# Conv sums in PSUM, weights' low parts and two conv tiles moved to GpSimd, in a one-core Conformer block

## The chip, the core and the metric

The kernel runs on one core of a Trainium2 chip. The core has a matrix engine (TensorE, in the profile PE, with its weight loads as PEld), a vector engine (VectorE, DVE), an activation engine (ScalarE, ACT), a general engine (GpSimd, POOL) and a queue engine that issues most of the transfers (SyncE, SP). Each works through its own queue in order and waits on semaphores for the others. Data lie in SBUF (128 partitions) and, for matrix results, in PSUM (8 banks of 128 x 512 float32). The metric is the device time of one execution, in microseconds.

## The reference

One layer of a block with two branches and a feed-forward part, sequence 1024, width 1024, all float32. What matters here is the convolution branch:

```python
def causal_depthwise_conv(u, w, b):
    width, ch = w.shape
    out = lax.conv_general_dilated(
        u, w[:, None, :].astype(u.dtype), window_strides=(1,), padding=[(width - 1, 0)],
        dimension_numbers=('NWC', 'WIO', 'NWC'), feature_group_count=ch)
    return out + b.astype(u.dtype)
...
        h = rms_norm(x, norm1_g[l])
        z = h @ w_in[l].astype(h.dtype)
        glu_in, q, k, v, gate_logits = jnp.split(z, SPLITS, axis=-1)

        a_val, a_gate = jnp.split(glu_in, 2, axis=-1)
        a = a_val * jax.nn.sigmoid(a_gate)
        a = causal_depthwise_conv(a, conv_w[l], conv_b[l])
        a = jax.nn.silu(rms_norm(a, conv_norm_g[l]))
        y_a = a @ w_conv_out[l].astype(a.dtype)
```

The convolution has 31 taps for each of 1024 channels. Beside it stand normalised queries and keys, attention in three dilated windows with 16 heads, gates that mix both branches, an output product, and a feed-forward part with a gated three-tap convolution.

## The kernel before

**Exact products from split numbers.** Every float32 matrix product is made of three products of rounded parts. A matrix is split by `split` (L76): ACT copies it into a rounded type (`hi`), DVE subtracts that from the source (`lo`), and the three matmuls hi·hi, hi·lo and lo·hi follow. A weight piece of 128 x 1024 goes through `wpiece` (L92): `stage` (L81) loads it through SP's queue into one of four `raw` buffers, `wsplit` (L86) writes it into one of four `whi` and one of four `wlo` buffers.

**Order of the work.** The program is written as a stream; the framework's planner (`schedule_with_timeline_sim=True`, L1278) orders the instructions of each engine in advance by durations of its own, earlier lines of the program first where several are ready. In blocks under `manual_schedule` (the start, L347, attention, L652, and part of the feed-forward part) ACT, DVE and PE keep the written order. Once planned, each engine's order is fixed.

**Stages.** (1) x is normalised, transposed and split into `hT` (L280 to L417). (2) GLU: for each of eight channel tiles c two products over `hT`, gate (`glug`) and value (`gluv`), each of two halves of 24 matmuls (`gemm_ch`, L115); ACT takes the sigmoid, DVE multiplies into `apad` (L445), a tile with 30 zero columns ahead. (3) q, k, v: six column groups `ch`, each with four weight pieces `qkv` (L512) and eight token tiles of 24 matmuls (`gemm_tok`, L120); for q and k `qkv_head` squares, sums and forms 1/sqrt (a power on POOL, L103, in `rstd_of`), DVE scales into `qn`, and `qkv_tail` transposes four blocks on PE (L496), splits and stores them. v is split and stored. (4) `cover` runs steps of the gate products (L542), (5) attention with the rest of the gate and conv-output products as filling between its steps (`fill`), (6) merge and output product, (7) feed-forward.

**The convolution** (`conv_branch`, L450) is written after the first `cover`, and what it needs is ready much earlier, so its instructions fill DVE's free places in stages 2 and 3. For each tile c: one `tensor_scalar` (L458, tap 0 with the bias) and thirty `scalar_tensor_tensor` (L461), each reading a shifted `apad` and the running sum `cacc`, both in SBUF. ACT then squares the finished tile (L468) and DVE adds it to `sqacc` (L469). When all eight are in, PE sums over channels (`pss`, L551), POOL forms the root (`crs`), PE spreads it (`psr`), DVE scales (L568), ACT takes the SiLU (L569), SP stores to `da` (L570). Attention's tiles (`p`, L589) lie where the convolution's tiles lay, so its first DVE step waits for that store.

**Buffers.** PSUM: pool `psA`, two tiles of two banks (`big_ps`), pool `psB`, four banks (`bank_ps`). GLU products and q/k transposes lie in `psA`, q/k/v and gate products in `psB`. SBUF: `apad` and `cacc` share ten buffers.

Of the kernel before, what the change touches and what calls it, by code (L numbers as in the profile page):

```python
# [13 lines left out]
F32 = mybir.dt.float32  # L14
F32R = mybir.dt.float32r
AF = mybir.ActivationFunctionType
# [5 lines left out]
P = 128  # L22
# [14 lines left out]
SHARE = 0.6  # L37
COVER = (24, 8, 20)


# [12 lines left out]
def block_kernel(ctx: ExitStack, tc: tile.TileContext, x, g1, g2, pack, mask,  # L53
# [21 lines left out]

    def split(hi, lo, src):  # L76

        act.activation(hi, src, AF.Copy)  # L78
        dve.tensor_tensor(out=lo, in0=src, in1=hi.bitcast(F32), op=ALU.subtract)  # L79

# [4 lines left out]

    def wsplit(src, name):  # L86
        hi = wp.tile([P, 1024], F32R, tag="whi", bufs=4, name=f"hi_{name}")[:, : src.shape[1]]
        lo = wp.tile([P, 1024], F32R, tag="wlo", bufs=4, name=f"lo_{name}")[:, : src.shape[1]]
        split(hi, lo, src)
        return hi, lo  # L90

    def wpiece(src, name, raw=None):  # L92
        raw = stage(src, name) if raw is None else raw
        hi, lo = wsplit(raw, name)
# [20 lines left out]
    def gemm_ch(ps, w, actT):  # L115
        for half in range(2):
            for _ in gemm_half(ps[:, half * 512 : half * 512 + 512], w, actT, half):
                pass
# [160 lines left out]
    with tc.tile_pool(name="ph1", bufs=1) as p1:  # L279
# [4 lines left out]
        for tt in range(8):  # L284
            xx = p1.tile([P, CW - 1 + T], F32, tag="apad", bufs=10, name=f"x_{tt}")[:, 0:T]
# [138 lines left out]
        with tc.issue_after(ends[0].ins), tc.issue_after(ends[1].ins):  # L424
            wsecond = [wpiece(w_ch[9], "g1"), wpiece(w_ch[1], "v1")]


        apad = []
        for c in range(8):
            a = p1.tile([P, CW - 1 + T], F32, tag="apad", bufs=10, name=f"apad_{c}")  # L430
            pool.memset(a[:, : CW - 1], 0.0)
# [7 lines left out]
            else:  # L439
                gp = big_ps(f"glug_{c}")  # L440
                gemm_ch(gp, wsecond[0] if c == 1 else wpiece(w_ch[8 + c], f"g{c}"), hT)
                act.activation(sg, gp, AF.Sigmoid)
                vp = big_ps(f"gluv_{c}")
                gemm_ch(vp, wsecond[1] if c == 1 else wpiece(w_ch[c], f"v{c}"), hT)
                dve.tensor_tensor(out=a[:, CW - 1 :], in0=vp, in1=sg, op=ALU.mult)  # L445
            apad.append(a)

        sqacc = p1.tile([P, T], F32, tag="sqacc", bufs=1, name="sqacc")

        def conv_branch():  # L450
            accs = []
            for c in range(8):
                acc = p1.tile([P, CW - 1 + T], F32, tag="apad", bufs=10, name=f"cacc_{c}")[:, 0:T]
                a = apad[c]
                w = lambda j: pk[:, C_CW + c * CW + j : C_CW + c * CW + j + 1]
                for j in range(CW):
                    if j == 0:
                        dve.tensor_scalar(acc, a[:, 0:T], w(0), pk[:, C_CB + c : C_CB + c + 1],  # L458
                                          op0=ALU.mult, op1=ALU.add)
                    else:  # L460
                        dve.scalar_tensor_tensor(out=acc, in0=a[:, j : j + T], scalar=w(j), in1=acc,  # L461
                                                 op0=ALU.mult, op1=ALU.add)
                accs.append(acc)
                if c == 0:
                    act.activation(sqacc, acc, AF.Square)
                else:
                    sq = p1.tile([P, T], F32, tag="csq", bufs=1, name=f"csq_{c}")
                    act.activation(sq, acc, AF.Square)  # L468
                    dve.tensor_tensor(out=sqacc, in0=sqacc, in1=sq, op=ALU.add)  # L469
            return accs  # L470
# [100 lines left out]
        cover(COVER[2])  # L571


# [708 lines left out]
```

## Time and profile before

| what | value |
|---|---|
| median of the runs | 1763.09 us |
| lowest and highest of 3 | 1762.22 and 1764.61 us |
| profiled execution, first to last instruction | 1761.6 us |
| median less that span | 1.5 us |
| matmuls | 8248 |
| HBM traffic | 154 GB/s over the span |

The profile gives the profiled execution by its span; the time around it isn't given apart, and the difference from the median, 1.5 us, is taken for it. The stages in time (us from the span's start): start 0 to 42, GLU 42 to 194, q/k/v 194 to 470, gate products alone 470 to 513, attention 513 to 895, merge and output product 895 to 1075, feed-forward to the end.

In a list of groups a row has the line, the engine, the operation, what it writes and reads, the count, then busy us and mean ns of one, then the engine's idle time just before. In a table by stretches of time a cell is the engine's busy us and, in brackets, its instructions. In a timeline the first two columns are start and duration in us. A matmul's duration contains latency that overlaps with the next matmul, so its rate is read from the distance between starts.

### The profile page before, as it was taken

To read this page: it belongs to the slowest core of one execution; us is meant where nothing else is said; L and a number is where in the kernel's file an instruction comes from. 1 tells how busy PE (TensorE), PEld (TensorE's weight loads), DVE (VectorE), ACT (ScalarE), POOL (GpSimd) and SP (SyncE) were. 2 spreads that over 40 slices of the span, in tenths; PEclk is the share of its full clock that TensorE was granted. 3 is DMA by queue.
4 is the path that set the end of the run, shared out by engine and by line. 5 is a ranking of instruction groups with operands and counts; after the bars stand their busy time and mean duration, and the time that the engine had idled before them with its cause. 6 is when DMAs were issued, how large, how long until landed. Compare 5 with 4: busy or idle time off the path is not lost.

```text
span 1761.6 us, 22662 instructions
## 1 busy us (share of the span) xinstructions
PE 1749.1 (99%) x8248; PEld 1454.3 (83%) x8248; DVE 1329.3 (75%) x1837; ACT 771.7 (44%) x1235; POOL 185.9 (11%) x193
## 2 busy tenths in 40 slices
PE   8999999999999999999999999999999999999999
PEld 6888888888888888888888888888888888888887
DVE  6999999999846666667655564687776777779863
ACT  6111132232256666667564343454544544534431
POOL 1000133034012222222210000000000000000000
PEclk9999999999999999999999999999999999999999
DMA  5111145344585655568446567532222222498851
GB/s 208 48 48 49 42 138 164 123 132 139 179 273 157 179 159 159 161 180 244 139 138 227 173 233 279 207 124 84 84 84 84 77 91 84 128 341 320 292 174 48
DMA packets 146530, 272.79 MB, mean 155 GB/s; under 512 B 11761, under 2 KB 61041, under 8 KB 146418
## 3 DMA queue, kind: packets, MB, share of 16 engines
q1 hardware_dynamic: 145264, 269.24, 47.2%
q10 hardware_dynamic: 1154, 2.10, 0.3%
q8 instruction: 65, 1.06, 0.2%
q14 instruction: 47, 0.39, 0.1%
HBM read 197.90 MB, written 73.40 MB: 154 GB/s over the span
## 4 chain that ended last, share of the span: by engine, by line
PE 93%; DMA 4%; DVE 1%; issue 1%; ACT 1%; SPq 0%; ACTq 0%; DVEq 0%
PE dx L1118 6%; PE xz L850 6%; PE xz L851 6%; PE xz L852 6%; PE qkv L129 5%; PE qkv L127 5%; PE qkv L128 5%; PE dy L1118 4%; PE pp L607 3%; PE gate L110 3%; PE gate L112 3%; PE gate L111 3%; PE y L850 2%; PE y L851 2%; PE y L852 2%; PE o L622 2%
## 5 line engine op out<-in xcount | busy, mean ns | idle before, releaser
L461 DVE SCALAR_TENSOR_TENSOR cacc<-apad,pk,cacc 128x1024 f32<-128x1024 f32 x240 | 299.7, 1288 | 0.7
L79 DVE TENSOR_TENSOR pl<-pp,ph 128x512 fp32r<-128x512 f32 x192 | 100.8, 553 | 88.1 <-ACT ph L78 87.9
L127 PE MATMUL qkv<-hi_qkv,hT 128*128 128x512 f32 x384 | 151.8, 396 | 0.0
L129 PE MATMUL qkv<-hi_qkv,hT 128*128 128x512 f32 x384 | 150.2, 391 | 0.0
L128 PE MATMUL qkv<-lo_qkv,hT 128*128 128x512 f32 x384 | 149.3, 389 | 0.0
L78 ACT ACTIVATE ph<-pp 128x512 fp32r<-128x512 f32 x192 | 87.1, 488 | 121.0 <-PE pp L607 120.3
L592 DVE CUSTOM_DVE_ANT_0 p<-s,m 128x128 f32<-128x128 f32 (+7 forms) x128 | 96.5, 754 | 53.3 <-PE s L588 41.4
L601 POOL TENSOR_SCALAR p<-p,st 128x128 f32<-128x128 f32 (+7 forms) x128 | 97.1, 758 | 315.7 <-DVE st L600 218.7
L1021 DVE SCALAR_TENSOR_TENSOR u<-u,pk 128x1023 f32<-128x1023 f32 x88 | 112.4, 1279 | 1.0 <-ACT u L1019 0.7
L103 POOL TENSOR_TENSOR rs<-ss,mhalf 128x8 f32<-128x8 f32 x32 | 75.0, 2348 | 337.6 <-DVE ss L102 337.6
L110 PE MATMUL gate<-hT,hi_gt 128*128 128x512 f32 x256 | 103.0, 402 | 0.0
L597 ACT ACTIVATE p<-p,st 128x128 f32<-128x128 f32 (+7 forms) x128 | 99.3, 775 | 5.5 <-DVE st L592 4.6
L111 PE MATMUL gate<-hT,hi_gt 128*128 128x512 f32 x256 | 100.3, 392 | 0.0
L112 PE MATMUL gate<-hT,lo_gt 128*128 128x512 f32 x256 | 100.1, 392 | 0.0
L129 PEld LDWEIGHTS qkv<-hi_qkv,hT 128*128 128x128 f32 x384 | 72.1, 188 | 15.3
L79 DVE TENSOR_TENSOR lo_uv<-raw_uv,hi_uv 128x1024 fp32r<-128x1024 f32 x20 | 24.5, 1226 | 79.5 <-ACT hi_uv L78 79.5
L128 PEld LDWEIGHTS qkv<-lo_qkv,hT 128*128 128x128 f32 x384 | 72.2, 188 | 14.3
L607 PE MATMUL pp<-ident,p 128*128 128x128 f32 x576 | 83.8, 272 | 0.0
L127 PEld LDWEIGHTS qkv<-hi_qkv,hT 128*128 128x128 f32 x384 | 72.2, 188 | 13.9
L607 PEld LDWEIGHTS pp<-ident,p 128*128 128x128 f32 x576 | 70.1, 140 | 15.3
L621 PE MATMUL o<-ph,v 128*128 128x512 f32 x192 | 74.8, 393 | 0.7 <-DVE op L633 0.7
L850 PE MATMUL xz<-blk_t,hi_s3g 128*128 128x512 f32 x176 | 68.6, 390 | 0.7 <-ACT xc L995 0.7
(309 smaller groups left out, 4638.8 us busy)
## 6 DMA issues: line engine op xcount, KB each, us to landing
wr<-w_down SPq DMA_DIRECT2D x45, 512.0 KB, 5.5
gr<-dff SPq DMA_DIRECT2D x62, 256.0 KB, 5.2
raw_qkv<-w_qkv SPq DMA_DIRECT2D x24, 512.0 KB, 3.8
dff<-u SPq DMA_DIRECT2D x22, 512.0 KB, 2.6
raw_uv<-w_up SPq DMA_DIRECT2D x21, 512.0 KB, 3.2
raw_ug<-w_up SPq DMA_DIRECT2D x20, 512.0 KB, 3.2
dv<-v SPq DMA_DIRECT2D x16, 512.0 KB, 3.2
raw_gt<-w_ch SPq DMA_DIRECT2D x16, 512.0 KB, 5.2
```

The costliest lines, as they stand in the source:

```text
L110: pe.matmul(o, hi[:, k, :], ah[:, k, :], start=(k == 0), stop=False)
L111: pe.matmul(o, hi[:, k, :], al[:, k, :], start=False, stop=False)
L112: pe.matmul(o, lo[:, k, :], ah[:, k, :], start=False, stop=(k == KT - 1))
L127: pe.matmul(ps, ah, hi[:, k % 2, :], start=(k == 0), stop=False)
L128: pe.matmul(ps, ah, lo[:, k % 2, :], start=False, stop=False)
L129: pe.matmul(ps, al, hi[:, k % 2, :], start=False, stop=(k == KT - 1))
L461: dve.scalar_tensor_tensor(out=acc, in0=a[:, j : j + T], scalar=w(j), in1=acc, op0=ALU.mult, op1=ALU.add)
L607: pe.transpose(pp[:, qb * P : (qb + 1) * P], pts[qb][:, kt * P : (kt + 1) * P], ident)
L850: pe.matmul(o, wh[:, k, :], bh[:, k, :], start=(start and k == 0), stop=False, skip_group_check=not start)
L851: pe.matmul(o, wh[:, k, :], bl[:, k, :], start=False, stop=False, skip_group_check=not start)
L852: end = pe.matmul(o, wl[:, k, :], bh[:, k, :], start=False, stop=(k == 3), skip_group_check=not start)
L1118: pe.matmul(banks[n], a[:, c], b[:, d], start=(start and i == 0 and m == 0), stop=(stop and i == nf - 1 and m == 2), skip_group_check=True)
```

## The change

The running sum of a conv tile moves from SBUF to a PSUM tile `work` of two banks (new pool `psC`, one buffer); the last tap writes the finished tile back over `apad`. For tiles 2 and 5 (`BY_POOL`) ACT makes the tap products (62 in all, alternating between two SBUF buffers) and POOL adds them (60 sums) to `part`. The squares go into `work`, or into a product buffer for tiles 2 and 5, in place of `csq`. The low parts of the weights of the GLU tiles 1 to 7 (14 pieces) and of q, k, v (24 pieces) are subtracted on POOL in place of DVE. The GLU products move from `psA` to the four banks of `psB`, and their sigmoid and product are done by halves. After the GLU stage `psA` is closed; its four banks go to `psC` (two) and `psT` (two tiles of one bank, for the q/k transposes), and are opened again as `psA2` for what follows. `apad` has eight buffers in place of ten.

```diff
+BY_POOL = (2, 5)
...
-    psA = ctx.enter_context(tc.tile_pool(name="psA", bufs=2, space=PSUM))
     psB = ctx.enter_context(tc.tile_pool(name="psB", bufs=4, space=PSUM))
+    psA_cm = tc.tile_pool(name="psA", bufs=2, space=PSUM, reuse_waits="tile")
+    psA = psA_cm.__enter__()
...
-    def split(hi, lo, src):
+    def split(hi, lo, src, by=dve):
 
         act.activation(hi, src, AF.Copy)
-        dve.tensor_tensor(out=lo, in0=src, in1=hi.bitcast(F32), op=ALU.subtract)
+        by.tensor_tensor(out=lo, in0=src, in1=hi.bitcast(F32), op=ALU.subtract)
...
-            wsecond = [wpiece(w_ch[9], "g1"), wpiece(w_ch[1], "v1")]
+            wsecond = [wpiece(w_ch[9], "g1", by=pool), wpiece(w_ch[1], "v1", by=pool)]
...
-                gp = big_ps(f"glug_{c}")
-                gemm_ch(gp, wsecond[0] if c == 1 else wpiece(w_ch[8 + c], f"g{c}"), hT)
-                act.activation(sg, gp, AF.Sigmoid)
-                vp = big_ps(f"gluv_{c}")
-                gemm_ch(vp, wsecond[1] if c == 1 else wpiece(w_ch[c], f"v{c}"), hT)
-                dve.tensor_tensor(out=a[:, CW - 1 :], in0=vp, in1=sg, op=ALU.mult)
+                gp = [bank_ps(f"glug_{c}_{half}") for half in range(2)]
+                gemm_ch(gp, wsecond[0] if c == 1 else wpiece(w_ch[8 + c], f"g{c}", by=pool), hT)
+                vp = [bank_ps(f"gluv_{c}_{half}") for half in range(2)]
+                gemm_ch(vp, wsecond[1] if c == 1 else wpiece(w_ch[c], f"v{c}", by=pool), hT)
+                for half in range(2):
+                    cs = slice(half * 512, half * 512 + 512)
+                    act.activation(sg[:, cs], gp[half], AF.Sigmoid)
+                    dve.tensor_tensor(out=a[:, CW - 1 + half * 512 : CW - 1 + half * 512 + 512],
+                                      in0=vp[half], in1=sg[:, cs], op=ALU.mult)
...
+        psA_cm.__exit__(None, None, None)
+        psC_cm = tc.tile_pool(name="psC", bufs=1, space=PSUM, reuse_waits="tile")
+        psC = psC_cm.__enter__()
+        psT_cm = tc.tile_pool(name="psT", bufs=2, space=PSUM, reuse_waits="tile")
+        psT = psT_cm.__enter__()
...
             accs = []
+            part = p1.tile([P, T], F32, tag="part", name="part")
+            prods = [p1.tile([P, T], F32, tag=t, name=f"prod_{t}") for t in ("prod", "csq")]
             for c in range(8):
-                acc = p1.tile([P, CW - 1 + T], F32, tag="apad", bufs=10, name=f"cacc_{c}")[:, 0:T]
                 a = apad[c]
+                acc = a[:, CW - 1 :]
                 w = lambda j: pk[:, C_CW + c * CW + j : C_CW + c * CW + j + 1]
...
+                bias = pk[:, C_CB + c : C_CB + c + 1]
+                if c in BY_POOL:
+                    act.activation(part, a[:, 0:T], AF.Identity, scale=w(0), bias=bias)
+                    for j in range(1, CW):
+                        act.activation(prods[j % 2], a[:, j : j + T], AF.Copy, scale=w(j))
+                        pool.tensor_tensor(out=acc if j == CW - 1 else part, in0=prods[j % 2], in1=part, op=ALU.add)
+                    work = prods[0]
+                else:
+                    work = psC.tile([P, T], F32, tag="C", name=f"work_{c}")
+                    dve.tensor_scalar(work, a[:, 0:T], w(0), bias, op0=ALU.mult, op1=ALU.add)
+                    for j in range(1, CW):
+                        dve.scalar_tensor_tensor(out=acc if j == CW - 1 else work, in0=a[:, j : j + T], scalar=w(j),
+                                                 in1=work, op0=ALU.mult, op1=ALU.add)
                 accs.append(acc)
                 if c == 0:
                     act.activation(sqacc, acc, AF.Square)
                 else:
-                    sq = p1.tile([P, T], F32, tag="csq", bufs=1, name=f"csq_{c}")
-                    act.activation(sq, acc, AF.Square)
-                    dve.tensor_tensor(out=sqacc, in0=sqacc, in1=sq, op=ALU.add)
+                    act.activation(work, acc, AF.Square)
+                    dve.tensor_tensor(out=sqacc, in0=sqacc, in1=work, op=ALU.add)
...
-            pt = big_ps(f"qt_{ch}_{tt}")[:, 0:512]
+            pt = psT.tile([P, 512], F32, tag="qt", name=f"qt_{ch}_{tt}")
...
-            wpieces = [wpiece(w_qkv[kind * 2 + g8, :, 2 * j : 2 * j + 2, :], f"qkv{ch}_{j}") for j in range(4)]
+            wpieces = [wpiece(w_qkv[kind * 2 + g8, :, 2 * j : 2 * j + 2, :], f"qkv{ch}_{j}", by=pool) for j in range(4)]
...
+    psT_cm.__exit__(None, None, None)
+    psC_cm.__exit__(None, None, None)
+    psA = ctx.enter_context(tc.tile_pool(name="psA2", bufs=2, space=PSUM, reuse_waits="tile"))
```

More of the change, by code (lines that the diff above doesn't have):

```diff
@@ L84, in stage, with wsplit, wpiece @@
         return raw
-    def wsplit(src, name):
+    def wsplit(src, name, by=dve):
         hi = wp.tile([P, 1024], F32R, tag="whi", bufs=4, name=f"hi_{name}")[:, : src.shape[1]]
         lo = wp.tile([P, 1024], F32R, tag="wlo", bufs=4, name=f"lo_{name}")[:, : src.shape[1]]
-        split(hi, lo, src)
+        split(hi, lo, src, by)
         return hi, lo
-    def wpiece(src, name, raw=None):
+    def wpiece(src, name, raw=None, by=dve):
         raw = stage(src, name) if raw is None else raw
-        hi, lo = wsplit(raw, name)
+        hi, lo = wsplit(raw, name, by)
         if len(src.shape) == 3:
@@ L116, in gemm_ch @@
         for half in range(2):
-            for _ in gemm_half(ps[:, half * 512 : half * 512 + 512], w, actT, half):
+            for _ in gemm_half(ps[half], w, actT, half):
                 pass
@@ L284, in block_kernel @@
         for tt in range(8):
-            xx = p1.tile([P, CW - 1 + T], F32, tag="apad", bufs=10, name=f"x_{tt}")[:, 0:T]
+            xx = p1.tile([P, CW - 1 + T], F32, tag="apad", bufs=8, name=f"x_{tt}")[:, 0:T]
             sp.dma_start(xx, x[tt * P : (tt + 1) * P, :])
@@ L424, in block_kernel @@
         with tc.issue_after(ends[0].ins), tc.issue_after(ends[1].ins):
-            wsecond = [wpiece(w_ch[9], "g1"), wpiece(w_ch[1], "v1")]
+            wsecond = [wpiece(w_ch[9], "g1", by=pool), wpiece(w_ch[1], "v1", by=pool)]
         apad = []
         for c in range(8):
-            a = p1.tile([P, CW - 1 + T], F32, tag="apad", bufs=10, name=f"apad_{c}")
+            a = p1.tile([P, CW - 1 + T], F32, tag="apad", bufs=8, name=f"apad_{c}")
             pool.memset(a[:, : CW - 1], 0.0)
```

7 lines of the change are left out of this document (removed).

## The prediction

> **What bounds the kernel now.** I read the busy shares of the page first.
>
> ```profile
> span 1761.6 us, 22662 instructions
> PE 1749.1 (99%) x8248; PEld 1454.3 (83%) x8248; DVE 1329.3 (75%) x1837; ACT 771.7 (44%) x1235; POOL 185.9 (11%) x193
> ```
>
> PE has 12.5 us without work in the whole span; no change can give back more unless it removes matmuls or raises their rate, and this one does neither. Next come the stretches of time of the GLU stage, of q/k/v and of the gate products before attention (columns PE, PEld, DVE, ACT, POOL).
>
> ```profile
> 44.00:194.00 150.00, 150.00 (x664) 124.24 (x663) 144.57 (x122) 22.40 (x23) 0.00 (x0) 1.00 0.15 50
> 194.00:470.00 276.00, 276.00 (x1280) 228.18 (x1278) 270.46 (x314) 75.66 (x111) 75.02 (x32) 1.00 0.42 130
> 470.00:513.00 43.00, 42.86 (x207) 35.75 (x205) 25.36 (x36) 19.20 (x25) 1.64 (x1) 1.00 0.96 295
> ```
>
> DVE is full in the first two, 415.0 of 426 us, but PE is too. A busy PE may hide waits, since durations overlap, so I take the rate from the timeline: first and last of 33 matmuls in a row, then four rows around a batch of transposes.
>
> ```profile
> 439.81 0.39 PE L129 MATMUL qkv<-hi_qkv,hT 128*128 128x512 f32 x1
> ...
> 447.06 0.39 PE L128 MATMUL qkv<-lo_qkv,hT 128*128 128x512 f32 x1
> ```
> ```profile
> 241.18 0.39 PE L127 MATMUL qkv<-hi_qkv,hT 128*128 128x512 f32 x1
> 241.41 0.60 PE L496 MATMUL qt<-ident,qn 128*128 128x128 f32 x4
> 241.76 0.48 PE L127 MATMUL qkv<-hi_qkv,hT 128*128 128x512 f32 x1
> 242.08 0.40 PE L128 MATMUL qkv<-lo_qkv,hT 128*128 128x512 f32 x1
> ```
>
> 32 steps in 7.25 us are 0.2266 us each; a batch of four transposes delays the next full-rate matmul by 242.08 - 241.41 - 0.23 = 0.44 us. q/k/v has 6 x 8 x 24 = 1152 matmuls and 32 batches: 261.0 + 14.1 = 275.1 of 276 us. Nothing is hidden there. Last, PE's waits: ten rows in the whole trace, of which these are the first, the seventh and the last; between 40 and 600 us the seventh is the only one.
>
> ```profile
> PE gb L350 <- DMA g1r<-g: 2.2, 1, 2.2
> ...
> PE s L587 <- DVE st L592: 0.6, 1, 0.6
> ...
> PE tp L321 <- DVE st L102: 0.2, 1, 0.2
> ```
>
> So the stage that the change touches has 0.6 us to give, at attention's first score. DVE is full there only because the conv fills every place that is left.
>
> **What the change takes off DVE, and what that is worth.** These groups show the conv sums, the first taps and the low parts.
>
> ```profile
> L461 DVE SCALAR_TENSOR_TENSOR cacc<-apad,pk,cacc 128x1024 f32<-128x1024 f32 x240 | 299.7, 1288 | 0.7
> L458 DVE TENSOR_SCALAR cacc<-apad,pk 128x1024 f32<-128x1024 f32 x8 | 6.5, 814 | 0.0
> L79 DVE TENSOR_TENSOR lo_qkv<-raw_qkv,hi_qkv 128x1024 fp32r<-128x1024 f32 x24 | 29.4, 1229 | 0.3 <-ACT hi_qkv L78 0.3
> L79 DVE TENSOR_TENSOR lo_g<-raw_g,hi_g 128x1024 fp32r<-128x1024 f32 x7 | 8.6, 1224 | 4.6 <-ACT hi_g L78 4.6
> L79 DVE TENSOR_TENSOR lo_v<-raw_v,hi_v 128x1024 fp32r<-128x1024 f32 x7 | 8.5, 1220 | 1.5 <-ACT hi_v L78 1.5
> ```
>
> Off DVE go 60 x 1.288 + 2 x 0.81 = 79 us of two conv tiles and 29.4 + 8.6 + 8.5 = 46.5 us of low parts: 126 us, so 415 becomes 289 of 426 us. On the path that sets the end this is worth nothing, because PE works beside it all the time.
>
> **Sums in PSUM.** No DVE instruction of the trace writes PSUM. Two that read bear on it.
>
> ```profile
> L501 DVE SCALAR_TENSOR_TENSOR ql<-qt,qkg,qh 128x512 fp32r<-128x512 f32 x16 | 12.1, 754 | 0.0
> L79 DVE TENSOR_TENSOR lo_s<-raw_uv,hi_s 128x512 fp32r<-128x512 f32 x20 | 13.8, 691 | 0.5
> ```
>
> Another 512 elements cost 1229 - 691 = 538 ns in SBUF; 754 + 538 = 1292 ns, the 1288 of the sum in SBUF. I take no extra cost. Bounds: nothing, or 0.5 us on each of 180 sums, 90 us, which leaves DVE at 379 of 426 us. A first tap into PSUM lies between 0.81 and 1.29 us: at most 6 x 0.48 = 3 us on DVE. Both are hidden by DVE's new spare time.
>
> **GLU by halves, transposes in `psT`.** Each of the four banks is written for 24 x 0.227 = 5.4 us and wanted again 16 us later, against one sigmoid and one product; the transposes keep two buffers. No matmul is added. Zero, covered as long as ACT and DVE are less than some 10 us late.
>
> **What a sum or a low part costs on POOL.** The trace has no two-input POOL operation of this size. The nearest rows: a one-input one, and the power of 128x8 under a busy DVE (32 of them, min/median/max) and alone.
>
> ```profile
> L601 POOL TENSOR_SCALAR p<-p,st 128x1024 f32<-128x1024 f32 x16 | 18.1, 1129 | 11.9 <-DVE st L600 11.5 <-PE pp L607 0.4
> L103 POOL TENSOR_TENSOR rs<-ss,mhalf x32: 1631/2537/3735, 209.2 to 435.8; 128x8 f32<-128x8 f32 x32
> L103 POOL TENSOR_TENSOR crs<-css,mhalf 128x8 f32<-128x8 f32 x1 | 1.6, 1641 | 49.4 <-DVE css L102 49.4
> ```
>
> Below it can't be cheaper than one input, 1.13 us; above, two readings are 2.26 us and waiting out one DVE operation adds 1.28: 3.5 us. I take 2.3 us: it is the one-input row twice, and the conv sums, the operations of which DVE has most, no longer read two SBUF tensors. That something on DVE holds POOL up is shown: the same power takes 1.64 us alone and 2.54 us in the middle of conv sums.
>
> The Trainium skill (SBUF — State Buffer, section Who interferes with whom) says that a DVE instruction with two SBUF inputs contends with a GpSimd instruction that reads SBUF, and one with at most one doesn't. By that rule the sums in PSUM free POOL and 2.3 us stands; were the hold-up to stay, 2.3 + 0.9 = 3.2 us would apply, which is the second rival below. The power's two times agree with the rule, but no run here yet shows POOL beside sums in PSUM. The Trainium skill (GPSIMD Engine Reference, section Performance versus the Vector engine) gives 4497 ns for a two-input add of 2048 elements; half, 2.25 us, is an estimate from that page, and by it the sums below would be the same within 2%.
>
> **Does the conv still end in time?** Tile c's `apad` is ready 21.8 us after that of tile c - 1, from the first and the last of seven starts; before, the last square was added at 481.8 us and attention's first score stood on it 31.6 us later.
>
> ```profile
> L445 DVE TENSOR_TENSOR apad<-gluv,sg x7: 1224/1226/1227, 63.6 to 194.2; 128x1024 f32<-128x1024 f32 x7
> ```
> ```profile
> 480.61 1.23 DVE L469 TENSOR_TENSOR sqacc<-sqacc,csq 128x1024 f32<-128x1024 f32 x1 [1.19 <-ACT csq L468]
> ```
> ```profile
> 513.41 0.44 PE s L587
> ```
>
> POOL starts tile 2 at 63.6 + 21.8 + 1.2 = 87 us. Two low parts per 21.8 us leave it 79%: 30 x 2.3 = 69 us of sums take 87 us, to 174; by 194, 16 us of tile 5 are done. In q/k/v POOL owes 24 x 2.3 + 75 (powers) = 130 of 276 us, so 53% is left: the other 53 us take 100, to 294. Tile 7 waits for that: `psC` has one buffer, tile 6's squares leave it only after tile 5's are added. Tile 7 is 31 x 1.29 = 40 us, at the share of DVE left beside other work; in q/k/v 138 conv sums of 174.5 us stood in DVE's 270.5.
>
> ```profile
> L461 DVE SCALAR_TENSOR_TENSOR cacc<-apad,pk,cacc 128x1024 f32<-128x1024 f32 x138 | 174.5, 1291 | 0.2
> ```
>
> 270.5 - 174.5 - 29.4 = 67 us, 24%; so 53 us, and the conv ends near 347 us, 135 us earlier than before. ACT's 62 products, at the 1.06 us of an `hi` to the 1.24 us of an activation with scale and bias, are 66 to 77 us beside 98 busy of 426. The early end takes away the wait of 0.6 us before attention; late next is PE itself.
>
> **The switches of weights.** What is queued behind the low parts on POOL is the power, and behind that `qn` and a bank of `psB`, which is wanted 17 us after its tile; square, sum, power, `qn` and four low parts ahead are about 0.6 + 0.7 + 2.4 + 0.7 + 9.2 = 13.6 us, covered. Raw buffers come free up to 10 us later; SP's next loads, and the stores queued behind them, have the 45 us to the next switch. The tightest place is the change from one group's four weight pieces to the next, five times. The first one, engine by engine:
>
> ```profile
> 235.48 1.06 ACT L78 ACTIVATE hi_qkv<-raw_qkv 128x1024 fp32r<-128x1024 f32 x1 [0.78 <-PE qkv L129]
> ```
> ```profile
> 245.23 1.23 DVE L79 TENSOR_TENSOR lo_qkv<-raw_qkv,hi_qkv 128x1024 fp32r<-128x1024 f32 x1
> ```
> ```profile
> 249.83 0.39 PE L129 MATMUL qkv<-hi_qkv,hT 128*128 128x512 f32 x1
> 250.06 0.39 PE L128 MATMUL qkv<-lo_qkv,hT 128*128 128x512 f32 x1
> ```
>
> The last low part ends at 246.46; PE, which had gone on with other token tiles, takes up the postponed matmul (a `lo` behind an `hi·lo` row, out of the usual turn) at 250.06. On POOL the first may wait 2.3 us for a running conv sum, then four follow with a power of about 2 us between: 236.6 + 2.3 + 9.2 + 2 = 250.1. Level, in a plan that is made anew around POOL. I cost it at 0.
>
> **Sum**: 0 - 0.6 us on the span, 1761.0; with the 1.5 us by which the median exceeds it, 1762.5; leaving half a microsecond for small slips at the switches, 1763.0.
>
> **Rivals.** A, *slower: low parts late at the switches.* The plan is fixed by the planner's durations; where POOL is slower than planned, the late low part holds PE, and on ACT a product that waits for its buffer holds `hi` parts and squares queued behind it. It decides from 2.3 us: at 2.8 us the last low part comes at 236.6 + 5 x 2.8 + 2 = 252.6, 2.5 us late, five times: +12.7, 1775.7. At 3.5 us, 6 us five times: 1793. For it: no slack at 2.3 by my sum. Against: 3.6 us of slack in the old order, and other token tiles to work on. B, *slower: POOL's conv tiles late.* Threshold: tile 5 by 427 us. From 87 us POOL has 340 us for 60 sums, 30 low parts and 64 us of powers: 3.1 us each. At 3.5 tile 5 ends near 490, the conv near 535: +53, 1816. C, *faster by over 0.2%* (3.5 us): would need a wait that I've shown not to exist, PE's 0.6; the waits outside lie at the start, behind attention and at the end, under a written order that stays: 1759 at best. That the offload does nothing because DVE never bound is the forecast itself.
>
> **How the numbers follow.** What a measurement here tells from no change is about 0.2%, 3.5 us. Forecast (same, 1760 to 1766.6): 0.66. A: 0.23, mostly 1767 to 1776. B: 0.06. C: 0.05. The range 1760 to 1776 takes in the forecast and A up to 2.8 us; outside are B, A at its upper bound, and C.
>
> **What would show it.** In the changed profile: PE at 276 of 276 us in q/k/v (wrong if PE waits for POOL or ACT at the switches); POOL's sums near 2.3 us (wrong above 2.8); the power near 1.64 us between sums; DVE near 290 of 426 us; the last square added near 350 us (wrong past 480). The forecast falls if the sum of PE's waits between 44 and 513 us exceeds 3.5 us.

## The result, and the profile after

| | before | after |
|---|---|---|
| median of the runs | 1763.24 us (1762.22 to 1764.61, 4 runs) | 1776.13 us (1775.7 to 1777.36, 4 runs) |
| profiled execution, span | 1761.6 us | 1774.0 us |

The changed kernel is slower by 12.9 us; the ratio is 1.0074, with an interval of 1.0062 to 1.0087. The forecast was 1763.0 us. Line numbers below are those of the changed kernel unless another is named: the split is L81, the head norm's sum, scaling, power and product are L502, L104, L105 and L505, the transposes L513, the conv's GpSimd sums L473, its VectorE sums L479, the first scores L606 and L607, the first step of the softmax L611.

First the page of the changed kernel.

```profile
span 1774.0 us, 22784 instructions
...
PE 1752.1 (99%) x8248; PEld 1456.9 (82%) x8248; DVE 1244.3 (70%) x1744; ACT 839.5 (47%) x1304; POOL 398.4 (22%) x291
```

VectorE lost 85 us of work, GpSimd gained 212, and PE, with the same 8248 matmuls, has 22 us without work in place of 12.5. Two stretches of time, and the first three of PE's waits, say where.

```profile
44.00:194.00 150.00, 150.00 (x664) 124.19 (x663) 135.71 (x113) 65.67 (x68) 111.07 (x47) 1.00 0.15 50
194.00:470.00 276.00, 268.84 (x1236) 221.08 (x1235) 201.60 (x237) 97.51 (x129) 167.03 (x81) 0.99 0.41 126
```
```profile
PE qt L513 <- DVE qn L505: 4.8, 3, 2.2
PE s L606 <- DVE st L611: 3.0, 1, 3.0
PE qkv L130 <- POOL lo_qkv L81: 2.4, 2, 2.2
```

The GLU stage is untouched. q/k/v, full before, now has 7.2 us in which PE stands still. The waits are of three kinds, and only the third is a loss that the prediction had weighed. Waiting is not all: adding up, over the whole trace, by how much each matmul starts later than the usual distance of its shape gives some 12.3 us more after than before, which is the 12.4 us of span. Of these 9.9 us lie between 220 and 308 us and some 3.3 between 484 and 528; the start and the end gave back 1.

**The first kind: a tiny VectorE operation held by GpSimd.** The timeline of VectorE around the second stop, then GpSimd's and PE's (start and duration in us):

```profile
243.36 1.28 DVE L479 SCALAR_TENSOR_TENSOR work<-apad,pk,work 128x1024 f32<-128x1024 f32 x1
244.54 2.06 DVE L104 TENSOR_SCALAR ss<-ss 128x8 f32<-128x8 f32 x1
246.51 0.68 DVE L505 TENSOR_TENSOR qn<-qkv,rs 128x512 f32<-128x512 f32 x1
```
```profile
242.57 1.66 POOL L105 TENSOR_TENSOR rs<-ss,mhalf 128x8 f32<-128x8 f32 x1
244.19 2.39 POOL L81 TENSOR_TENSOR lo_qkv<-raw_qkv,hi_qkv 128x1024 fp32r<-128x1024 f32 x1
```
```profile
245.32 0.39 PE L129 MATMUL qkv<-hi_qkv,hT 128*128 128x512 f32 x1
247.34 0.52 PE L513 MATMUL qt<-ident,qn 128*128 128x128 f32 x3 [1.63 <-DVE qn L505]
```

The scaling of 8 numbers per partition, 0.17 us as a rule, starts at 244.54 while GpSimd's low part runs, and ends at 246.60, when that ends (244.19 + 2.39 = 246.58). The power that `qn` needs had been ready at 244.23; but `qn` stands behind the next tile's scaling in VectorE's queue, so it starts at 246.51, and PE's transposes wait for it. The longest of the `qt` waits, 2.15 us at 269 us, has the same picture. The third, 1.0 us at 303 us, has another: the scaling is done at 294.2, and its power starts only at 298.9, behind a sum and a low part in GpSimd's queue. The lines of the group, before and after, then the sum of squares just ahead of the scaling (minimum, median and maximum in ns):

```profile
L102 DVE TENSOR_SCALAR ss<-ss 128x8 f32<-128x8 f32 x32 | 5.8, 182 | 0.0
```
```profile
L473 POOL TENSOR_TENSOR part<-prod_csq,part 128x1024 f32<-128x1024 f32 x30 | 74.0, 2466 | 1.3
...
L81 POOL TENSOR_TENSOR lo_qkv<-raw_qkv,hi_qkv 128x1024 fp32r<-128x1024 f32 x24 | 57.2, 2406 | 28.1 <-ACT hi_qkv L80 28.1
...
L105 POOL TENSOR_TENSOR rs<-ss,mhalf 128x8 f32<-128x8 f32 x32 | 52.6, 1645 | 55.3 <-DVE ss L104 54.8
...
L104 DVE TENSOR_SCALAR ss<-ss 128x8 f32<-128x8 f32 x32 | 17.8, 558 | 0.1
```
```profile
L502 DVE TENSOR_REDUCE ss<-sq x32: 671/683/690, 205.9 to 435.7; 128x8 f32<-128x512 f32 x32
```

The mean of the scaling is three times what it was; 12 of the 32 last over 0.25 us, 8 of these beside a sum and 4 beside a low part. GpSimd's own wait of 54.8 us for the scaling (the end of its row) is no loss of this kind: all but some 5 us of it lie behind its last sum, which ends at 314 us, where it has little else to do, and before the change it was 337.6 us. The Trainium skill (SBUF — State Buffer, section Who interferes with whom) has this: a `tensor_scalar` may take the pair of ports that VectorE shares with GpSimd, and then whoever issues first keeps it for the whole instruction while the other stands still. The trace agrees, with 2.06 us in place of 0.17. Not every operation from SBUF to SBUF is held: the sum of squares never took over 690 ns, though 22 of the 32 ran beside GpSimd. The prediction drew on the same section for the sums. It gave the rule for at most one SBUF input without the exception for such forms, and did not ask which other VectorE operations fall under it.

**The second kind: the door of the attention.** The timeline of PE from the last gate product to the first scores:

```profile
521.86 0.39 PE L114 MATMUL gate<-hT,lo_gt 128*128 128x512 f32 x1
525.26 0.69 PE L606 MATMUL s<-kh,q 128*128 128x384 f32 x1 [3.02 <-DVE st L611]
525.75 0.52 PE L607 MATMUL s<-kl,q 128*128 128x384 f32 x1
526.07 0.63 PE L112 MATMUL gate<-hT,hi_gt 128*128 128x512 f32 x1
526.50 0.63 PE L113 MATMUL gate<-hT,hi_gt 128*128 128x512 f32 x1
```

PE stands for 3.0 us, 0.6 before. Behind that the matmuls come 0.43 us apart instead of 0.227, until 528.6 us: some 1.5 us more. What the softmax's first step (L611, at 524.91 us) waits for is the space of its tile; the profile puts this wait down to the load of `v`, and the store orders below show that it is the stores. In the program's addresses (bytes in a partition):

```
p_0_0   80896 to 81408
after:  apad_0  76800 to 81016   stored first
        apad_7  81024 to 85240   stored eighth, issued 517.85, landed 524.74
before: cacc_4  76800 to 81016   stored fifth,  issued 505.87, landed 512.89
        cacc_3  81024 to 85240   stored fourth
```

With fewer `apad` buffers the tile lies partly on the one that is stored last. So the wait of 0.6 us that the change was to remove became one of 3.0.

**The third kind: the first low part of a switch.** GpSimd's timeline at the first of the five changes of weights, and PE's:

```profile
235.38 2.44 POOL L473 TENSOR_TENSOR part<-prod_csq,part 128x1024 f32<-128x1024 f32 x1
237.90 2.41 POOL L473 TENSOR_TENSOR part<-prod_prod,part 128x1024 f32<-128x1024 f32 x1
240.26 2.37 POOL L81 TENSOR_TENSOR lo_qkv<-raw_qkv,hi_qkv 128x1024 fp32r<-128x1024 f32 x1
```
```profile
242.68 0.50 PE L130 MATMUL qkv<-lo_qkv,hT 128*128 128x512 f32 x1 [2.19 <-POOL lo_qkv L81]
```

The `hi` of this piece was ready at 236.85, but its low part stands behind two sums. Before, it ran on VectorE from 237.51 to 238.73. The prediction counted one sum ahead and looked at the last of the four low parts; it is the first that held PE. Three of the five changes lie behind GpSimd's last sum, and PE waits at none of them.

### The profile page after: what moved, and what is told of

The parts are those of the page before. It is cut to its first block, busy times and chain, and to the rows that moved or that the text cites. A ratio compares the mean times of both kernels' runs of the same rounds, so it can differ in the third digit from the quotient of the medians.

```text
span 1774.0 us, 22784 instructions
## 1 busy us (share of the span) xinstructions
PE 1752.1 (99%) x8248; PEld 1456.9 (82%) x8248; DVE 1244.3 (70%) x1744; ACT 839.5 (47%) x1304; POOL 398.4 (22%) x291
## 4 chain that ended last, share of the span: by engine, by line
PE 90%; DVE 4%; DMA 2%; POOL 1%; ACT 1%; issue 1%; SPq 0%; ACTq 0%; POOLq 0%; DVEq 0%
PE dx L1137 7%; PE xz L869 6%; PE xz L871 6%; PE xz L870 6%; PE dy L1137 5%; PE qkv L130 3%; PE qkv L131 3%; PE qkv L129 3%; PE pp L626 3%; PE gate L112 3%; PE gate L114 3%; PE gate L113 3%; PE y L869 2%; PE y L871 2%; PE y L870 2%; PE o L641 2%
## 5 line engine op out<-in xcount | busy, mean ns | idle before, releaser
L479 DVE SCALAR_TENSOR_TENSOR work<-apad,pk,work 128x1024 f32<-128x1024 f32 x174 | 223.8, 1286 | 4.0
L81 DVE TENSOR_TENSOR pl<-pp,ph 128x512 fp32r<-128x512 f32 x192 | 100.8, 553 | 88.3 <-ACT ph L80 88.0
L611 DVE CUSTOM_DVE_ANT_0 p<-s,m 128x128 f32<-128x128 f32 (+7 forms) x128 | 96.4, 754 | 57.3 <-PE s L607 43.4
L81 DVE TENSOR_TENSOR lo_uv<-raw_uv,hi_uv 128x1024 fp32r<-128x1024 f32 x20 | 24.5, 1226 | 80.0 <-ACT hi_uv L80 80.0
L473 POOL TENSOR_TENSOR part<-prod_csq,part 128x1024 f32<-128x1024 f32 x30 | 74.0, 2466 | 1.3
```

Of the source, the lines that this page charges most:

```text
L479: dve.scalar_tensor_tensor(out=acc if j == CW - 1 else work, in0=a[:, j : j + T], scalar=w(j), in1=work, op0=ALU.mult, op1=ALU.add)
```

## The experiments

Twelve kernels were run, each beside the kernel before on the same chip. "Scaling" is the head norm's L104.

| run | edit | median us | ratio to before (interval) |
|---|---|---|---|
| e1_affine_act | changed kernel, scaling on ScalarE | 1769.57 | 1.0036 (1.0023 to 1.0049) |
| e2_no_pool_tiles | changed kernel, no conv tiles on GpSimd | 1769.72 | 1.0033 (1.0021 to 1.0044) |
| e3_low_dve | changed kernel, low parts on VectorE | 1780.23 | 1.0093 (1.0078 to 1.0108) |
| e4_reverse_store | changed kernel, stores from tile 7 to 0 | 1775.83 | 1.0069 (1.0054 to 1.0084) |
| e8_store_order | changed kernel, stores 0, 7, 6 to 1 | 1771.49 | 1.0041 (1.0026 to 1.0056) |
| e9_affine_order | e1 and e8 together | 1765.6 | 1.0016 (1.0006 to 1.0026) |
| e10_affine_order_nopool | e1, e8 and e2 together | 1762.72 | 0.9994 (0.9985 to 1.0004) |
| e6_psum_only | neither low parts nor tiles on GpSimd | 1801.54 | 1.0211 (1.0196 to 1.0226) |
| e11_sums_sbuf_one | as e6, sums in one SBUF buffer | 1799.27 | 1.0206 (1.0191 to 1.0221) |
| e12_sums_sbuf_two | as e6, sums in two SBUF buffers | 1769.62 | 1.0037 (1.0023 to 1.0051) |
| e14_psum_two | as e6, two PSUM buffers | 1799.71 | 1.0208 (1.0193 to 1.0224) |
| e13_affine_two_input | changed kernel, scaling with two inputs | 1776.88 | 1.0078 (1.0063 to 1.0093) |

### Is it the held scaling?

```diff
-            rstd_of(rs, ss, DH, ss)
+            act.activation(ss, ss, AF.Copy, scale=1.0 / DH, bias=EPS)
+            pool.tensor_tensor(out=rs, in0=ss, in1=mhalf, op=ALU.pow)
```

> The mean with epsilon of the 32 head norms (128x8) is formed on ScalarE in place of VectorE. Theory 1 (while GpSimd runs a sum or a low part, VectorE's tiny 128x8 scaling waits for its end, 0.17 us becomes up to 2.06, and the row scaling behind it on VectorE comes late for the transposes): no hold on VectorE is left, the waits of the transposes (4.8 us, and the slow clock after one of them, 1.3 us) go mostly: 1770 to 1772 us. Theory 2 (GpSimd's queue alone makes the power late; the hold on VectorE costs nothing, since the power would wait for GpSimd anyway): 1775 to 1777 us, the waits of the transposes stay.

1769.57 us: 6.6 us of the 12.9 go with this one small operation, a little more than theory 1 had. In q/k/v PE works 273.75 of 276 us in place of 268.84. Its waits in that stage:

```profile
PE s L607 <- DVE st L612: 3.1, 1, 3.1
...
PE qkv L130 <- POOL lo_qkv L81: 2.0, 3, 0.9
...
PE qt L514 <- DVE qn L506: 0.2, 1, 0.2
```

The waits for `qn` fall from 4.8 to 0.2 us. GpSimd's low parts take what they took (2412 ns), so it was not their speed; the door, on the first row, is as it was. What is left are three waits for low parts, none over 0.9 us.

The other question was whether the two conv tiles on GpSimd are to blame.

```diff
-BY_POOL = (2, 5)
+BY_POOL = ()
```

> All eight conv tiles on VectorE with sums in PSUM; the low parts stay on GpSimd. Theory 1 (conv sums on GpSimd ahead of low parts and powers cause the stalls of q/k/v): the stage runs at full rate again (276 us for what took 285), what is left is the longer wait before attention (some 4 us with the slow clock): 1766 to 1768 us. Theory 3 (low parts on GpSimd are late by themselves, 2.4 us each against a release every 1.4 us): waits at all five switches, 1772 to 1780 us. Theory 4 (sums in PSUM or the smaller buffers cost the time): as the changed kernel, 1774 to 1778 us.

```profile
PE s L606 <- DVE st L611: 4.1, 1, 4.1
...
PE qt L513 <- DVE qn L505: 1.0, 1, 1.0
```

No wait for a low part is left, and one for `qn`: of the 7.2 us in q/k/v 1.0 remains. The low parts alone still hold the scaling 6 times in place of 12 (mean 377 ns against 558). So either edit, without the tiles on GpSimd or without the scaling on VectorE, takes away most of the loss in q/k/v: it needs both. The door got worse, and the time, 1769.72 us, lies 2 us above theory 1.

Would another form of the scaling on VectorE escape? With a tile of eps as the second input in place of a second constant:

```diff
+        epst = p1.tile([P, 8], F32, name="epst")
+        pool.memset(epst, EPS)
...
-            rstd_of(rs, ss, DH, ss)
+            dve.scalar_tensor_tensor(out=ss, in0=ss, scalar=1.0 / DH, in1=epst, op0=ALU.mult, op1=ALU.add)
+            pool.tensor_tensor(out=rs, in0=ss, in1=mhalf, op=ALU.pow)
```

> The changed kernel with the small scaling of the head norms still on VectorE, but written with two inputs (the sums of squares times 1/64, plus a tile that holds eps) in place of one input and two constants. Theory H1 (only the form with one SBUF input is held until GpSimd's running operation ends): its mean falls from 558 to under 250 ns with none over 0.5 us, the waits of qt for qn go as in the run with the scaling on ScalarE, and the time is 1769 to 1771 us. Rival H2 (any small VectorE operation from SBUF to SBUF is held beside GpSimd): mean over 450 ns, the longest about 2 us, 1775 to 1777 us. Between (two inputs share with GpSimd, as the low parts on VectorE did at 3.2 to 3.4 for 1.22 us): 250 to 450 ns, 1770 to 1773 us.

It does not: 1776.88 us, the waits for `qn` as in the changed kernel. VectorE's and GpSimd's timelines at the same place:

```profile
243.81 2.05 DVE L505 SCALAR_TENSOR_TENSOR ss<-ss,epst 128x8 f32<-128x8 f32 x1
```
```profile
243.43 2.41 POOL L81 TENSOR_TENSOR lo_qkv<-raw_qkv,hi_qkv 128x1024 fp32r<-128x1024 f32 x1
```

Again the end (245.86) is that of GpSimd's operation (245.84). H2 holds for both forms of the scaling that were tried, not for any operation from SBUF to SBUF: the sum of squares is free here too (at most 690 ns). A scaling that reads or writes PSUM was not tried.

### Low parts back on VectorE, the conv tiles left on GpSimd

```diff
-    wpiece(..., f"qkv{ch}_{j}", by=pool)
+    wpiece(..., f"qkv{ch}_{j}")
```

The four calls of the GLU stage lose `by=pool` too.

> The low parts go back to VectorE; tiles 2 and 5 stay on ScalarE and GpSimd. Theory 1: the wait for a low part (2.4 us) goes, the holds on VectorE's tiny scaling and with them waits of the transposes stay while GpSimd adds, which ends earlier without the low parts (near 260 us): 1769 to 1774 us. Theory 3: all stalls of q/k/v go: 1766 to 1768 us. Theory 4: 1774 to 1778 us.

Slower than the changed kernel by 4.1 us, which no theory had foreseen. Two things come together. On ScalarE (timeline) a weight's `hi` stands behind products that wait for a sum on GpSimd to free their buffer:

```profile
197.44 1.15 ACT L472 ACTIVATE prod_csq<-apad,pk 128x1024 f32<-128x1024 f32 x1 [1.36 <-POOL part L473]
199.90 1.15 ACT L472 ACTIVATE prod_prod<-apad,pk 128x1024 f32<-128x1024 f32 x1 [1.30 <-POOL part L473]
200.95 1.04 ACT L80 ACTIVATE hi_qkv<-raw_qkv 128x1024 fp32r<-128x1024 f32 x1
```

PE waits 3.2 us for it. And on VectorE two low parts, with both inputs in SBUF, beside GpSimd's sums:

```profile
247.85 1.21 DVE L81 TENSOR_TENSOR lo_qkv<-raw_qkv,hi_qkv 128x1024 fp32r<-128x1024 f32 x1
...
250.84 6.53 DVE L81 TENSOR_TENSOR lo_qkv<-raw_qkv,hi_qkv 128x1024 fp32r<-128x1024 f32 x2
```

Two take 6.53 us where one alone takes 1.21; GpSimd's sum in that time takes 3.28 in place of 2.4. The conflict goes both ways; in the changed kernel these 24 two-input operations no longer stand on VectorE, but the small scaling still does.

### Is it the store that the first tile waits for?

```diff
-        for c in range(8):
+        for c in reversed(range(8)):
```

> The last loop of the convolution (scale, SiLU, store) runs over the tiles from 7 to 0, nothing else. Theory 5 (attention's first score tiles lie on the space of the last conv tile, so they wait for the landing of the eighth store, where they waited for the fifth before): the wait before attention shrinks from 3.2 us to under 1 us and the slow clock after it goes, 1771 to 1773 us. Theory 6 (that wait is set by the late end of q/k/v and the transfers behind it, whatever the order): 1775 to 1777 us.

The wait stayed at 2.8 us, and the time, 1775.83 us, is that of theory 6. The account that the eighth store holds the door had failed as I put it. The addresses explain it: the tile lies on the end of tile 0 as well as on the beginning of tile 7, and reversed, tile 0 is stored last. An order that stores both first tests that:

```diff
-        for c in range(8):
+        for c in (0, 7, 6, 5, 4, 3, 2, 1):
```

> The changed kernel with one edit: the last conv loop takes the tiles in the order 0, 7, 6, 5, 4, 3, 2, 1. The first probability tile of the attention lies on the space of tiles 0 and 7, so that in the changed kernel it waits for the eighth store, which landed at 524.74 us, while PE could have begun at about 522. Theory S (the space decides): with these two tiles stored first (the second store landed at 516.18) the wait of 3.2 us on the first scores shrinks to 0 to 0.7 us, and the 1.4 to 1.5 us of slow matmuls behind it go too: 1776.1 less 4.0 to 4.7, so 1771.4 to 1772.1 us. Rival (the wait is set by the end of the stores as a whole, or by what the first scores' chain takes by itself): the wait stays at 3.0 us or more, 1775.5 to 1776.5 us. Rival 2 (the gap goes but the slow matmuls are not its result): 1772.9 to 1773.6 us.

1771.49 us, within theory S, 4.6 us less than the changed kernel. The timeline of PE at the door:

```profile
520.43 0.39 PE L114 MATMUL gate<-hT,lo_gt 128*128 128x512 f32 x1
520.66 0.33 PE L606 MATMUL s<-kh,q 128*128 128x384 f32 x1
520.83 0.34 PE L607 MATMUL s<-kl,q 128*128 128x384 f32 x1
521.01 0.40 PE L112 MATMUL gate<-hT,hi_gt 128*128 128x512 f32 x1
```

No stop, and no slow matmuls behind it; the order does matter, so theory 6 is out. Then both edits, and both with all conv tiles on VectorE:

> The changed kernel with two edits: the small scaling of the head norms on ScalarE in place of VectorE (as in the run with that edit alone, 1769.6 us, whose first scores still waited 3.2 us with 1.4 us of slow matmuls behind), and the order of stores 0, 7, 6, 5, 4, 3, 2, 1. Theory: the two losses have separate causes and add up, so that both edits give 1769.6 less 3.9 to 4.6, so 1765.0 to 1765.7 us; what is then left above the kernel before are waits for low parts of 2.0 us at weight switches. Rival (the losses are one: what is won in q/k/v is lost again at the door): 1768.5 us or more.

> The changed kernel with three edits: small scaling on ScalarE, stores in the order 0, 7, 6, 5, 4, 3, 2, 1, and all eight conv tiles on VectorE with sums in PSUM (the low parts stay on GpSimd). From the run with all tiles on VectorE (1769.7 us: one wait of 1.1 us in q/k/v, 4.2 us and 1.4 us of slow matmuls at the first scores). Theory: with these gone 1769.7 less 5.9 to 6.7, so 1763.0 to 1763.8 us, which is the time before: the sums in PSUM and the low parts on GpSimd then win nothing, since PE is full in this stage either way. Rival (the relieved VectorE is worth something once the two losses are gone): under 1761.5 us. Rival 2 (POOL's low parts cost PE by themselves at the switches): 1765 us or more, with waits for low parts of 2 us in all.

1765.6 us: the two losses add up (6.6 + 4.6 = 11.2 expected from the single edits, 10.5 measured). 1762.72 us without the tiles on GpSimd as well, where PE works all of q/k/v:

```profile
194.00:470.00 276.00, 276.00 (x1280) 228.43 (x1279) 258.93 (x267) 80.18 (x142) 101.97 (x53) 1.00 0.43 130
```

That can't be told from the kernel before: its median lies 1.2 us under that of the runs beside it, and the interval takes in 1. Once the losses are mended, low parts on GpSimd and sums in PSUM are worth nothing that can be told from zero. The two conv tiles on GpSimd still cost something: 1765.6 us is 0.16% above the kernel before, with an interval of 0.06 to 0.26%.

### What do the sums in PSUM do alone?

```diff
-BY_POOL = (2, 5)
+BY_POOL = ()
...
-    wpiece(..., by=pool)
+    wpiece(...)
```

The second edit stands for all five calls with `by=pool`. Left of the change are the PSUM sums, the buffers and the halves.

> The changed kernel with the low parts back on VectorE and all eight conv tiles on VectorE: left of the change are the sums in PSUM, the conv written back over its padded input, halves of the gated unit, and the pools of PSUM tiles. Theory S (the door is a matter of the space that the stores leave): no wait in q/k/v over 0.3 us, and at the first scores a wait of 3 to 4.2 us with 1.4 us of slow matmuls: 1767 to 1769 us. Rival (the door's wait comes from GpSimd's work or the low parts): the time before, 1762.5 to 1764 us. Rival 2 (the sums in PSUM cost VectorE or PE by themselves): over 1770 us, with VectorE's sums over 1350 ns.

1801.54 us, 33 us above theory S. The second rival's "over 1770" fits, but not its sign: the sums last 1286 ns, as before. No wait in q/k/v, but the last squares come late:

```profile
PE pss L570 <- DVE sqacc L486: 33.4, 1, 33.4
```

So the group's mean says nothing. The distance between starts does. VectorE's timeline of this run, three sums in a row of one tile:

```profile
124.33 3.93 DVE L479 SCALAR_TENSOR_TENSOR work<-apad,pk,work 128x1024 f32<-128x1024 f32 x3
```

(3.93 - 1.29) / 2 = 1.32 us from start to start. Now two stretches of the kernel before, seven sums each:

```profile
44.74 9.21 DVE L461 SCALAR_TENSOR_TENSOR cacc<-apad,pk,cacc 128x1024 f32<-128x1024 f32 x7
...
120.01 8.46 DVE L461 SCALAR_TENSOR_TENSOR cacc<-apad,pk,cacc 128x1024 f32<-128x1024 f32 x7
```

The same seven operations: 1.32 us apart in the first, (8.46 - 1.29) / 6 = 1.195 in the second. At 44 us only tile 0 is there; from 66 us on the planner alternates between two tiles. A sum that reads what the operation just ahead wrote begins after its end; one that doesn't begins 0.09 us before it. With one `work` buffer two tiles can't alternate. Is it that, or PSUM? One and two SBUF buffers, and two PSUM buffers:

```diff
-                    work = psC.tile([P, T], F32, tag="C", name=f"work_{c}")
+                    work = prods[0]
```
```diff
-                    work = psC.tile([P, T], F32, tag="C", name=f"work_{c}")
+                    work = prods[c % 2]
```
```diff
-        psC_cm = tc.tile_pool(name="psC", bufs=1, space=PSUM, reuse_waits="tile")
+        psC_cm = tc.tile_pool(name="psC", bufs=2, space=PSUM, reuse_waits="tile")
...
-            pt = psT.tile([P, 512], F32, tag="qt", name=f"qt_{ch}_{tt}")
+            pt = bank_ps(f"qt_{ch}_{tt}")
```

> The kernel of the run e6_psum_only (low parts and all conv tiles on VectorE, 1801.5 us, where the last sum came 33 us late for PE) with the conv's sums in one SBUF buffer in place of the one PSUM buffer. In that run a sum that follows another of the same tile starts 1.325 us after it, in the kernel before most start 1.196 us after the last one, though each lasts 1.286 to 1.288 us in both. Theory D (dependence: a sum that reads the one issued just before it starts 0.13 us later; in the kernel before two tiles alternate, with one buffer they cannot): the step stays at 1.32 us, and only the first taps get cheaper (0.81 for 1.34 us, 8 times: 4 us), so 1795 to 1799 us. Rival (PSUM: its sums can't overlap): the step falls to 1.196 us and the time to 1763 to 1769 us.

> As the run with one SBUF buffer, but two SBUF buffers that the tiles take by turns. Theory D: two tiles alternate again on VectorE, the step is 1.196 us, the last sum comes at about 482 to 486 us, no wait for it of over 1 us, and the time is 1763 us, or up to 1769 us with the wait at the first scores that the stores' order leaves (3.2 to 4.2 us and 1.4 us of slow matmuls in other runs). Rival (the conv written back over its padded input, or the halves of the gated unit, make VectorE late): the last sum stays after 510 us, and the time over 1790 us.

> As the run e6_psum_only, but two PSUM buffers for the sums (the transposes of q and k go to the shared PSUM tiles, to make room). Theory D: two tiles alternate, the step is 1.19 to 1.20 us in PSUM too, the last sum comes at 486 to 490 us (4.3 us of dearer first taps), and the time is 1763 to 1770 us, the wait at the first scores included. Rival (PSUM): the step stays at 1.325 us, the last sum after 510 us, 1795 to 1802 us. If the transposes' shared tiles cost PE, waits of qt or qkv for PSUM tiles show it.

VectorE's timelines: one SBUF buffer, two SBUF buffers, two PSUM buffers.

```profile
87.37 3.92 DVE L479 SCALAR_TENSOR_TENSOR prod_prod<-apad,pk,prod_prod 128x1024 f32<-128x1024 f32 x3
```
```profile
89.62 1.27 DVE L479 SCALAR_TENSOR_TENSOR prod_prod<-apad,pk,prod_prod 128x1024 f32<-128x1024 f32 x1
90.82 1.27 DVE L479 SCALAR_TENSOR_TENSOR prod_csq<-apad,pk,prod_csq 128x1024 f32<-128x1024 f32 x1
```
```profile
88.57 8.43 DVE L477 SCALAR_TENSOR_TENSOR work<-apad,pk,work 128x1024 f32<-128x1024 f32 x7
```

1.32, 1.20 and (8.43 - 1.28) / 6 = 1.19 us: it is the dependence, in PSUM and SBUF alike, and theory D is right on the step in all three. One SBUF buffer costs 1799.27 us, two 1769.62: 29.7 us for the second buffer. In the run with one, 122 sums follow a sum of the same tile directly, in the run with two 15; at 0.125 us the difference is 13 us. The rest goes with idle time of VectorE: from 44 us to the last square it stands 31.7 us with one buffer and 13.9 with two. Little of that is the wait for ScalarE's square at a tile's end (3.6 against 2.2 us); why the rest arose was not tried apart. On the time, theory D missed the first two runs by under 1 us and the third by 30, where the rival's time came out without the rival's step. There PE waits within q/k/v instead:

```profile
PE qkv L130 <- DVE lo_qkv L81: 8.7, 10, 1.0
PE qt L511 <- DVE qn L503: 7.3, 3, 5.2
PE qt L511 <- DVE ss L104: 6.7, 7, 2.1
```

VectorE had its last square added at 474 us, earlier than before (482), and in its queue more sums stood ahead of head norms and low parts. Why the plan came out so is open: the transposes' new place changed more than the buffer. Two SBUF buffers are 6.4 us over before without any wait in q/k/v; there PE put the first scores ahead of `pss` and waited 2.4 us for `kh` and `kl`, then 1.0 at the door.

## Why the prediction was wrong

- **What bounds the kernel: right.** PE was the bound, relief of VectorE was worth nothing, and the run with all losses mended (1762.72 us) agrees with the forecast of 1763.0 for a change that costs nothing, though it leaves the two conv tiles on VectorE; with them on GpSimd 1765.6 us is the least that was reached. What failed is the cost.
- **"The switches of weights ... covered ... I cost it at 0": the step that failed first.** It set 13.6 us for "square, sum, power, `qn`" and four low parts against a bank wanted 17 us after its tile. The chain was not longer than that: for the three tiles whose transposes PE waited for, square to end of `qn` took 12.4, 10.2 and 12.8 us, and before it had taken 8.1 to 17.3 us without a wait. But it was the transposes that wanted `qn` first, and the order made anew had drawn them nearer: from square to transposes the median of the 32 is 17.1 us before and 12.5 after, and PE came to these three 11.0, 8.2 and 11.9 us behind the square. The slack was gone, and what was late then cost time: above all the small scaling between sum and power, for which the prediction had no term. It took up to 2.06 us, 12 us more in all, and in the two longer waits it held the `qn` of another tile whose power was done. 6.6 us, by the run with the scaling on ScalarE. At the first low part 2.2 us of waiting came from two sums ahead where one had been counted. Why the planner drew the transposes nearer is open.
- **"The early end takes away the wait of 0.6 us before attention": wrong in place and sign.** The conv did end early (the last square added at 373 us), but scaling and stores stand behind `cover` steps and moved with the end of q/k/v: the eighth store was issued at 517.85. Which store the door needs was set by addresses, and the change had rearranged them. It cost 2.4 us more of waiting and 1.5 of slow matmuls; the run with the other order, which also loses the 0.6 us of before, is 4.6 us faster.
- **Rival A: the right number for mostly other reasons.** Its 1775.7 us stood on low parts of 2.8 us. They take 2.41 (predicted 2.3), and waits for low parts are 2.4 of 10.2 us in the three rows, at the first change of weights and hardly at the others, not five times. The half of it on ScalarE, products that hold `hi`, happened (at 237.85 us one that had waited 1.0 us for its buffer stands ahead of a `hi`), but no wait of PE is put down to it in the changed kernel; one is with the low parts on VectorE.
- **POOL's sums at 2.3 us, the power at 1.64: right.** 2405 to 2466 ns and 1645 ns, so sums in PSUM do leave GpSimd free, and rival B was out.
- **"Sums in PSUM ... I take no extra cost": right in duration, wrong in step.** 1286 ns against 1288, but 1.325 us apart in place of 1.196. The two rows of seven were in the trace of before, and I read the mean. In the changed kernel GpSimd's help hides it: VectorE has 337 of 426 us, where I had 289. Of these 48 us 12 are the held scaling, 7 the lost overlap (223.8 / 174 against 299.7 / 240 us on 180 sums) and 3 the first taps (1.35 us, just over my bound of 1.29). Some 20 more are counting: the 98 sums and low parts were taken off at full length though each overlapped its neighbour by 0.09 us, and in the old trace 4 low parts lay before 44 us and 5 sums behind 470. With neither tiles nor low parts on GpSimd the sums did set the end (33.4 us of waiting).
- **"The conv ends near 347 us": 373 us**, with no effect on the end.
- **The test was right.** "The forecast falls if the sum of PE's waits between 44 and 513 us exceeds 3.5 us": it was 7.2.

## What to carry to other kernels

Before moving work to GpSimd, list the VectorE operations that will run beside it and can meet it, the tiny ones above all (here those with two SBUF inputs and the `tensor_scalar` from SBUF to SBUF; not the sum of squares, nor sums with one input in PSUM), and look who stands behind each in VectorE's queue: 8 elements can wait as long as GpSimd's operation lasts. Slack read from the old order is not slack in an order that is made anew. When buffers are merged or their number is changed, look up whose space the next stage's first tile takes, and in which order that space is released. And price a chain of dependent operations by the distance of their starts, not by the mean of one: a buffer fewer can cost the alternation that hid it.

## What the runs showed of the hardware

- A VectorE scaling of 128x8 from SBUF to SBUF waits for the end of GpSimd's sum or low part of 128x1024 that runs already, in the form with one input (2.06 for 0.17 us) and in the one with two (2.05). Beside GpSimd's power of 128x8 it does not (0.16 us at 299.6 and 0.17 at 358.6 us), and the sum of squares, 128x512 to 128x8 from SBUF to SBUF, does not wait for either (671 to 690 ns). The one that reads PSUM (`css`) took 0.17 us, but no GpSimd operation ran beside it.
- A stop of PE can cost more than its length. The granted clock is recorded at half for 3.4 us after the 3.0 us at the door and after the 2.15 us at 269 us in the changed kernel; matmuls come 0.427 us apart for about 1.4 us of loss. The Trainium skill (TensorE: Matmul & The Clock Gate, section HAM oscillation — how this bites in real kernels) gives the rule to leave no idle gaps over some 3.4 us. Here shorter ones were enough, though not always: in the run with the stores 0, 7, 6 to 1 the same stop before 269 us had no slow matmuls behind it, and the 2.2 us stop before 243 us, which had none in the changed kernel, had the clock at half from 244.2 us.
- Dependent sums of 128x1024 on VectorE start 1.32 us apart, independent ones 1.195, in SBUF and PSUM, each 1.28 to 1.29 us long.
